# Another order for the first LayerNorms, v's products and the PSUM banks of an encoder layer on Trainium2

## The chip, the cores and the metric

The kernel runs on one core of a Trainium2 chip. The metric is the device time of one execution in microseconds (us), the median of several runs. The engines are TensorE (PE; its weight loads are listed as PEld), VectorE (DVE), ScalarE (ACT), GpSimd (POOL) and SyncE (SP), which issues nearly all of the DMAs. Each engine works through its own queue in order.

## The reference

One layer of a hybrid encoder on 1024 tokens of 1024 channels, all in fp32. What matters here is the beginning:

```python
h = layer_norm(x, emb_ln_g, emb_ln_b)
proj = h @ w_in                                 # [1024, 1024] x [1024, 5120]
q, k, v, z_a, u, z_b, g_a, g_b = split(proj)
attn = neighbourhood_attention(q, k, v, rpb)    # 8 heads x 64, window 8 x 16 on a 16 x 64 grid
u = centred_depthwise_conv(u, conv_w, conv_b)
h_lru = rg_lru(u, forward) + rg_lru(u, backward)
m = sigmoid(g_a + b0) * ((attn * silu(z_a)) @ w_ba) + sigmoid(g_b + b1) * ((h_lru * silu(z_b)) @ w_bb)
out = layer_norm(ALPHA * h + m @ w_out, ln_g, ln_b)
```

## The kernel before

Every product is done in fp32r with both operands split into a high and a low part: high x high, low x high, high x low, three matmuls for one. The order of the instructions is written out by hand for every engine: each queue gets its instructions in the order of the program text, and waits are put in where tiles are shared. So a line moved in the text moves all of its instructions in their queues.

The 1024 tokens are 8 tiles x0 to x7 of 128 tokens. A tile goes through these helpers, named as in the text:

- `load_x(i)`, `load_wv(c)`, `qk_load(m)`: DMAs, in SP's order, for x, for v's weights and for a 128-column block of the q and k weights.
- LayerNorm of tiles 0, 1 and 3: `ln_stats`, `ln_root` (a square root on ScalarE), then `ln_v(i, c)` for each half on VectorE, which reads the scale and offset straight from four PSUM banks `gps`. There they are spread over all partitions by `gb_spread`, 16 transposes of the column `gb_col`; that column comes from a transpose of the row `gb_row` (L409) and a ScalarE copy (L410). Tiles 2 and 4 to 7 take `ln_scale(i)` on ScalarE and `ln_g(i)` on GpSimd, four half-width operations, with the scale and offset copied from PSUM to SBUF by `gb_copy` on ScalarE.
- `turn(i, kk)`: four TensorE transposes (L270) of one half of tile i into a PSUM bank; `turn_hi` (L279, ScalarE) writes the high part of the turned block, `turn_lo` (L128, VectorE) the low part.
- `wv_hi(k)` (L195, ScalarE), `wv_lo(k)` (GpSimd): high and low part of chunk k of v's weights; `qk_prep(m)`: the same for q's weights (L171 on ScalarE, then GpSimd).
- `v_part(i, kind, ks)` (L328): v's products for tile i; kind "h" is high x high, "a" low x high, "w" high x low of the chunks `ks`. 24 of them make a tile's v. `v_hi` (L335) and `v_lo` read the result out, `v_store` stores it.
- `q_part(m, n)`: 24 products of a block of q; `q_hi` (L355, ScalarE) and `q_lo` (L360, VectorE) read it out. The block q(0,0) is special: its first 256 columns are computed early and its last 256 after v3, into the same bank, so the bank is held all that while.
- `t_full`, `t_last`, `t_hi`, `t_lo`: sums of turned blocks of tiles 4 to 7 for a Strassen-like scheme used later (product names a11, s2 and so on); VectorE, ScalarE and GpSimd.
- `warm_up(n)`: n idle products (L202) of a zero tile, which write into the bank `clock`; the three numbers of `WARM` say how many stand where.

The results of `turn`, `v_part` and `q_part` use four PSUM banks in this stage, and `bank(name)` hands them out in the order in which it is called:

```python
places = itertools.chain((0, 1, 2, 3, 0, 1, 2, 0, 2, 3, 1), itertools.cycle((2, 3, 0, 1)))
...
return ps0.tile([P, HALF], F32, tag=f"b{next(places)}", bufs=1, name=name)
```

A tile that gets a bank waits until the tile before it in that bank has been read for the last time. The turned blocks of tiles 2 to 7 use four other banks, which are the `gps` banks released.

The stage after it, unchanged in the text, is this (q(0,0)'s read-out and v4 are close to its end):

```python
    q_part(0, 0, slice(256, HALF))
    t_last(4)
    tile_in(5)
    q_hi(0, 0)
    ...
    tile_lo(5)
    q_lo(0, 0)
    q_store(0, 0)
    keep(7)
    q_part(1, 0)
    t_full(5)
    ...
    for kind in "hwa":
        v_part(4, kind, KS)
```

Then come v5 to v7, the rest of q, a softplus polynomial of `lru_lambda` on VectorE with one Exp on ScalarE (L629), and 16 pairs of column blocks, seven products each (up to about 424 us), with the convolution, the gates and the scans beside them; then attention, merge and output.

Of the kernel before, what the change touches and what calls it, by code (L numbers as in the profile page):

```python
# [28 lines left out]
N_PAIR = 16  # L29


WARM = 18, 4, 6
CONV_AT = (7, 24, 45, 66)
GATE_AT = (14, 24, 35, 45, 56, 66, 77, 87)
LATE_AT = (102, 102, 103, 104, 105)
# [32 lines left out]
def encoder_kernel(ctx, tc, x, gb1, gb, w_qk, w_v, w_s, w_ba, w_bb, w_gate, smalls, bias, w_out, out):  # L68
    nc = tc.nc
    V, A, G, PE, SP = nc.vector, nc.scalar, nc.gpsimd, nc.tensor, nc.sync  # L70
# [12 lines left out]
    hb12 = pool("hb12", "right")  # L83

    turns = []
    places = itertools.chain((0, 1, 2, 3, 0, 1, 2, 0, 2, 3, 1), itertools.cycle((2, 3, 0, 1)))

    def bank(name):
        if turns:
            return banks[0].tile([P, HALF], F32, tag=next(turns[0]), bufs=2, name=name)  # L90
        if banks[0] is ps0:
            return ps0.tile([P, HALF], F32, tag=f"b{next(places)}", bufs=1, name=name)
        return banks[0].tile([P, HALF], F32, tag="bank", name=name)
# [12 lines left out]
    ident = cst.tile([P, P], F32, name="ident")  # L106
# [20 lines left out]
    def lo_of(eng, lo, full, hi):  # L127
        eng.tensor_tensor(lo, full, hi.bitcast(F32), ALU.subtract)  # L128
# [28 lines left out]
    gb_row = hts[2].tile([16, P], F32, tag="ht1h", name="gb_row")  # L157
    gb_col = hts[2].tile([P, 16], F32, tag="ht1l", name="gb_col")
    zero = wsp.tile([P, P], mybir.dt.bfloat16, tag="a21", name="zero")
    V.memset(zero[:], 0.0)  # L160
    clock = bank("clock")
# [7 lines left out]
    def qk_hi(m):  # L169
        qk_w[m] = pair(wpl, [P, NK, P], f"wqk{m}", tag="w", bufs=2)  # L170
        A.copy(qk_w[m][0][:], qk_s[m][:])  # L171

    def qk_lo(m):
        hi, lo = qk_w[m]
        lo_of(G, lo[:], qk_s.pop(m)[:], hi[:])

    def qk_prep(m):
        qk_hi(m)
        qk_lo(m)
# [3 lines left out]
    def load_x(i):  # L183
        xs[i] = ln.tile([P, D], F32, tag="x", bufs=5, name=f"x{i}")
        if i == 0:
            for sl in halves:
                SP.dma_start(xs[i][:, sl], x[i][:, sl])
        else:
            SP.dma_start(xs[i][:], x[i])
# [4 lines left out]
    def wv_hi(k):  # L194
        A.copy(wv[0][k][:], wvs[k // 4][:, k % 4, :])  # L195

    def wv_lo(k):
        lo_of(G, wv[1][k][:], wvs[k // 4][:, k % 4, :], wv[0][k][:])

    def warm_up(n):  # L200
        for _ in range(n):
            PE.matmul(clock[:, :P], zero[:], zero[:], start=True, stop=True)  # L202

    gps = [[psg.tile([P, HALF], F32, name=f"gps{z}{c}") for c in range(2)] for z in range(2)]
    halves = [slice(c * HALF, (c + 1) * HALF) for c in range(2)]

    def gb_spread(z, c):

        for k in range(4):
            r = 8 * z + 4 * c + k  # L210
            PE.transpose(gps[z][c][:, k * P:(k + 1) * P], gb_col[:, r:r + 1].to_broadcast([P, P]), ident[:])

    def gb_copy(z, c):
        A.copy(gb_t[z][c][:], gps[z][c][:])

    def ln_stats(i):
        st, mv, e = (ln.tile([P, n], F32, tag=f"ln{n}{c}", bufs=2, name=f"ln{i}{c}")
                     for n, c in ((12, "t"), (2, "m"), (4, "e")))
        sts[i] = st, mv, e[:, 3:4], e[:, 0:3]
        sd, ve = sts[i][2:]  # L220
        for c in range(2):
            V.bn_stats(st[:, 6 * c:6 * c + 6], xs[i][:, halves[c]])
        V.bn_aggr(mv[:], st[:].rearrange("p (c s) -> p c s", c=2))
        V.tensor_scalar(ve[:, 0:1], mv[:, 1:2], EPS, -0.5, ALU.add, ALU.mult)

    def ln_root(i):
        st, mv, sd, ve = sts[i]
        A.activation(sd, mv[:, 1:2], AF.Sqrt, bias=eps_t[:])

    def ln_sums(i):  # L230
        ln_stats(i)
        ln_root(i)

    def ln_rstd(i):
        st, mv, sd, ve = sts[i]
        V.reciprocal(sd, sd)
        V.tensor_scalar(ve[:, 1:2], sd, sd, ve[:, 0:1], ALU.mult, ALU.mult)
        V.tensor_scalar(sd, ve[:, 1:2], 1.5, sd, ALU.add, ALU.mult)

    def ln_v(i, c):  # L240

        z, (st, mv, sd, ve), sl = xs[i], sts[i], halves[c]
        V.scalar_tensor_tensor(z[:, sl], z[:, sl], mv[:, 0:1], gps[0][c][:], ALU.subtract, ALU.mult)
        if c == 0:
            ln_rstd(i)
        V.scalar_tensor_tensor(z[:, sl], z[:, sl], sd, gps[1][c][:], ALU.mult, ALU.add)

    def ln_scale(i):

        z, (st, mv, sd, ve) = xs[i], sts[i]  # L250
        ln_rstd(i)
        V.tensor_scalar(ve[:, 2:3], mv[:, 0:1], -1.0, sd, ALU.mult, ALU.mult)
        A.activation(z[:], z[:], AF.Identity, bias=ve[:, 2:3], scale=sd)

    def ln_g(i):
        z = xs[i]
        for c in range(2):
            for w, op in enumerate((ALU.mult, ALU.add)):
                G.tensor_tensor(z[:, halves[c]], z[:, halves[c]], gb_t[w][c][:], op)

    def keep(i):
        SP.dma_start(h_d[i], xs[i][:])
# [3 lines left out]
    def turn(i, kk):  # L266
        tp = tps[i, kk] = bank(f"tp{i}_{kk}")
        for k4 in range(4):
            k = 4 * kk + k4
            PE.transpose(tp[:, k4 * P:(k4 + 1) * P], xs[i][:, k * P:(k + 1) * P], ident[:])  # L270

    def ti(i):
        return slice((i % 4) * P, (i % 4 + 1) * P)

    def tp4(i, kk):
        return tps[i, kk][:].rearrange("p (k t) -> p k t", k=4)

    def turn_hi(i, kk):
        A.copy(blocks[kk][i // 4][0][:, :, ti(i)], tp4(i, kk))  # L279

    def turn_lo(i, kk):
        hi, lo = blocks[kk][i // 4]
        lo_of(V, lo[:, :, ti(i)], tp4(i, kk), hi[:, :, ti(i)])
# [38 lines left out]
    def v_part(i, kind, ks):  # L322

        if i not in vos:
            vos[i], vn[i] = bank(f"v{i}"), 0
        for k in ks:
            a = blocks[k // 4][i // 4][kind == "a"][:, k % 4, ti(i)]
            PE.matmul(vos[i][:], a, wv[kind == "w"][k][:], start=vn[i] == 0, stop=vn[i] == 23)  # L328
            vn[i] += 1
# [3 lines left out]
    def v_hi(i):  # L333
        vs = outs["v", i] = ln.tile([P, H, 2, DH], F32R, tag="vs", bufs=2, name=f"vs{i}")
        A.copy(vs[:, :, 0, :], vos[i][:].rearrange("p (h d) -> p h d", d=DH))  # L335
# [11 lines left out]
    def q_part(m, n, cols=slice(0, HALF)):  # L347
        if (m, n) not in qos:
            qos[m, n] = bank(f"q{m}_{n}")
        run(mm3(qos[m, n][:, cols], [([t[:, 4 * kk + k, :] for t in qk_w[m]], [t[:, k, cols] for t in blocks[kk][n]])  # L350
                                     for kk in range(2) for k in range(4)]))
# [41 lines left out]
    K0, K1, KS, BOTH = range(4), range(4, 8), range(8), range(2)  # L393
# [12 lines left out]
    SP.dma_start(sm[:], smalls)  # L406

    warm_up(WARM[0])
    PE.transpose(clock[:, 256:272], gb_row[:], ident[:16, :16])  # L409
    A.copy(gb_col[:], clock[:, 256:272])  # L410
    warm_up(WARM[1])
    for z, c in ((0, 0), (1, 0), (0, 1), (1, 1)):
        gb_spread(z, c)
    warm_up(WARM[2])
    ln_sums(0)
    ln_v(0, 0)
    turn(0, 0)
    warm_up(WARM[2])
    wv_hi(0)
# [2 lines left out]
    ln_v(0, 1)  # L422
    keep(0)
    load_x(5)
    turn(0, 1)
    warm_up(WARM[2])
    wv_hi(2)
    wv_hi(3)
    turn_hi(0, 1)
    turn_lo(0, 0)  # L430
    gb_copy(0, 0)
    wv_hi(4)
    wv_hi(5)
    ln_sums(1)
    turn_lo(0, 1)
    wv_hi(6)
    wv_hi(7)
    gb_copy(1, 0)
    for k in KS:
        wv_lo(k)  # L440
    qk_prep(0)
    for k in K0:
        v_part(0, "h", (k,))
        v_part(0, "a", (k,))
    v_part(0, "w", (0, 1))
    v_part(0, "h", (4, 5))
    v_part(0, "w", (2, 3))
    v_part(0, "h", (6, 7))
    v_part(0, "a", K1)
    ln_v(1, 0)  # L450
    ln_v(1, 1)
    keep(1)
    qk_load(1)
    load_x(6)
    turn(1, 0)
    turn_hi(1, 0)
    v_part(0, "w", (4, 5))
    v_part(1, "h", K0)
    turn(1, 1)
    for z in BOTH:  # L460
        gb_copy(z, 1)
    turn_hi(1, 1)
    v_part(0, "w", (6, 7))
    ln_stats(2)
    turn_lo(1, 0)
    ln_root(2)
    v_hi(0)
    ln_scale(2)
    turn_lo(1, 1)
    ln_g(2)  # L470
    v_part(1, "w", K0)
    v_part(1, "h", K1)
    v_part(1, "a", KS)
    v_part(1, "w", K1)
    ln_sums(3)
    q_part(0, 0, slice(0, 256))
    ln_v(3, 0)
# [525 lines left out]
    for slot in range(7 * N_PAIR + 4):  # L1003
        p, k = divmod(slot, 7)
# [183 lines left out]
    for unit in range(-NT, H * NT + PV_LAG):  # L1188
        h, c = divmod(unit, NT)
# [162 lines left out]
    for i in range(NT):  # L1352
        last = i == NT - 1
        load_z(i + 3)
        z = zs.pop(i)
# [115 lines left out]
```

## Time and profile before

| | us |
|---|---|
| median of 3 runs (678.39 to 678.75) | 678.40 |
| the profiled execution | 678.46 |
| its span in the profile | 676.7 |
| TensorE busy | 665.2 (98%) |
| VectorE / ScalarE / GpSimd busy | 492.7 / 364.5 / 355.8 |
| first product of v starts | 9.99 |
| q's first half ends | 26.48 |
| first product of v4 starts | 49.19 |

All times in the rows are counted from the start of the span. A row of a timeline or of the chain gives start, duration, engine, source line, operation, tiles (out<-in, buffer numbers left out), and in brackets the idle time of that engine just before and what ended it. Matmuls are pipelined, so the durations of neighbours overlap and their pace is read from group lengths.

### The profile page before, as it was taken

How to read it: one execution, taken by the hardware profiler on the slowest of the kernel's cores; microseconds unless marked ns; L12 is line 12 of the kernel's file. 1: busy time of each engine (PE TensorE's matmuls, PEld its weight loads, DVE VectorE, ACT ScalarE, POOL GpSimd, SP SyncE). 2: the span in 40 equal slices, each digit the busy share in tenths (PEclk: the TensorE clock that was granted, in tenths of full speed). 3: DMA queues.
4: the chain of work that ended last, by engine and by line, in shares of the span. 5: the costliest groups of instructions: out<-in, count | busy, mean ns of one | idle time of the engine just before them, and what ended most of it. 6: DMA issues, size and time to landing. Idle time of an engine off the chain costs nothing.

```text
span 676.7 us, 9344 instructions
## 1 busy us (share of the span) xinstructions
PE 665.2 (98%) x3201; PEld 555.7 (82%) x3201; DVE 492.7 (73%) x821; ACT 364.5 (54%) x612; POOL 355.8 (53%) x258
## 2 busy tenths in 40 slices
PE   8999999999999999999999999999999999999995
PEld 6888888888888887888788888888888878888884
DVE  6978747886998699879967785477787787443434
ACT  6554433256786676669576634477777554210110
POOL 6798632434677576567647444116155456334442
PEclk9999999999999999999999999999999999999998
DMA  8654353233434133431553456998793467412211
GB/s 326 244 179 170 122 206 126 77 110 123 125 128 144 40 103 115 170 126 48 195 178 122 173 191 254 316 366 296 255 323 132 162 220 281 178 62 94 93 63 62
DMA packets 48702, 113.39 MB, mean 168 GB/s; under 512 B 5056, under 2 KB 9744, under 8 KB 47120
## 3 DMA queue, kind: packets, MB, share of 16 engines
q1 hardware_dynamic: 48624, 112.81, 47.2%
q8 instruction: 25, 0.41, 0.3%
q14 instruction: 21, 0.17, 0.1%
q10 hardware_dynamic: 32, 0.01, 0.0%
HBM read 77.11 MB, written 35.68 MB: 167 GB/s over the span
## 4 chain that ended last, share of the span: by engine, by line
PE 89%; DVE 6%; DMA 2%; issue 1%; SPq 1%; ACT 0%; POOL 0%; DVEq 0%; POOLq 0%
PE a L134 30%; PE o L134 13%; PE mb L134 12%; PE s L134 11%; PE q L134 6%; PE v L328 6%; PE acc L1107 3%; PE s L1061 3%; PE pt L1083 3%; PE g L759 2%; DMA wqk_s<-in_w_qk_dram 2%; DVE ws_l L128 1%; PE tp L270 1%; DMA rsb<-rs_d 1%; DVE uc L717 1%
## 5 line engine op out<-in xcount | busy, mean ns | idle before, releaser
L134 PE MATMUL o<-wo_h,ml 128*128 128x512 f32 (+1 forms) x136 | 51.2, 377 | 0.0
L134 PE MATMUL o<-wo_l,mh 128*128 128x512 f32 (+1 forms) x136 | 51.2, 376 | 0.0
L134 PE MATMUL o<-wo_h,mh 128*128 128x512 f32 (+1 forms) x136 | 51.2, 376 | 0.0
L134 PE MATMUL a<-ht_h,ws_h 128*128 128x512 f32 x128 | 50.0, 390 | 0.0
L134 PE MATMUL a<-ht_l,ws_h 128*128 128x512 f32 x128 | 49.8, 389 | 0.0
L134 PE MATMUL a<-ht_h,ws_l 128*128 128x512 f32 x128 | 49.8, 389 | 0.0
L134 PE MATMUL a<-b_h,wa_h 128*128 128x512 f32 x128 | 49.8, 389 | 0.0
L134 PE MATMUL a<-b_h,wa_l 128*128 128x512 f32 x128 | 49.8, 389 | 0.0
L134 PE MATMUL a<-b_l,wa_h 128*128 128x512 f32 x128 | 49.8, 389 | 0.0
L1071 DVE CUSTOM_DVE_ANT_0 sc<-s,bias 128x384 f32<-128x384 f32 (+1 forms) x64 | 33.4, 522 | 21.6 <-PE s L1061 14.2
L1361 DVE SCALAR_TENSOR_TENSOR z<-z,o 128x512 f32<-128x512 f32 (+1 forms) x17 | 11.2, 656 | 51.0 <-PE o L134 51.0
L1091 ACT CAST pt_h<-pt 128x384 fp32r<-128x384 f32 x64 | 29.0, 453 | 25.3 <-PE pt L1083 17.3
L1371 POOL TENSOR_TENSOR z<-z,gb 128x1024 f32<-128x1024 f32 x7 | 16.8, 2400 | 48.5 <-ACT z L1370 48.5
L1076 ACT ACTIVATE p<-sc,summ 128x384 f32<-128x384 f32 (+1 forms) x64 | 37.8, 591 | 5.5 <-DVE summ L1071 5.3
L1340 ACT ACTIVATE sd<-mv,eps_z 128x1 f32<-128x1 f32 x8 | 2.4, 294 | 67.1 <-DVE mv L1366 67.1
L128 DVE TENSOR_TENSOR pt_l<-pt,pt_h 128x384 fp32r<-128x384 f32 x64 | 33.2, 519 | 2.1 <-ACT pt_h L1091 1.6
L328 PE MATMUL v<-wv,b_h 128*128 128x512 f32 x128 | 32.9, 398 | 0.6 <-ACT b_h L279 0.5
L867 POOL CAST wb_h<-wb 128x512 fp32r<-128x512 f32 x9 | 7.0, 779 | 47.4 <-DMA wb<-in_w_bb_dram 47.4
L1061 PE MATMUL s<-ks,qs 128*128 128x384 f32 (+1 forms) x128 | 31.4, 327 | 0.0
L1083 PEld LDWEIGHTS pt<-ident,p 128*128 128x128 f32 x176 | 23.1, 140 | 8.5
L1083 PE MATMUL pt<-ident,p 128*128 128x128 f32 x176 | 29.6, 272 | 0.0
L128 POOL TENSOR_TENSOR wb_l<-wb,wb_h 128x512 fp32r<-128x512 f32 x16 | 22.0, 1375 | 14.3 <-ACT wb_h L865 13.6
(438 smaller groups left out, 2204.2 us busy)
## 6 DMA issues: line engine op xcount, KB each, us to landing
ks<-k_d SPq DMA_DIRECT2D x8, 1024.0 KB, 7.5
h_d<-x SPq DMA_DIRECT2D x8, 512.0 KB, 5.0
v_d<-vs SPq DMA_DIRECT2D x8, 512.0 KB, 3.7
q_d<-q SPq DMA_DIRECT2D x8, 512.0 KB, 3.1
ga_d<-ga SPq DMA_DIRECT2D x16, 256.0 KB, 2.2
gb_d<-gb SPq DMA_DIRECT2D x16, 256.0 KB, 2.6
k_d<-k SPq DMA_DIRECT2D x8, 512.0 KB, 3.4
qs<-q_d SPq DMA_DIRECT2D x8, 512.0 KB, 5.5
```

The source lines that it names most:

```text
L128: eng.tensor_tensor(lo, full, hi.bitcast(F32), ALU.subtract)
L134: PE.matmul(o, a, b, start=first and i == 0, stop=last and i == len(prods) - 1, skip_group_check=not (first and last))
L328: PE.matmul(vos[i][:], a, wv[kind == "w"][k][:], start=vn[i] == 0, stop=vn[i] == 23)
L759: PE.matmul(o[:, n, :], w[:, 2 * d + b, :], us[b][:, n * HALF:(n + 1) * HALF], start=z == 0, stop=z == 1)
L1061: PE.matmul(o[:, :P * len(near(t))], q[:, t * P:(t + 1) * P], k[:, z, keys], start=z == 0, stop=z == 1)
L1071: V.tensor_tensor_reduce(s[:, :w], o[:, :w], heads[h][2][:, b0:b0 + w], -1.0, 3.0e38, ALU.add, ALU.min, accum_out=sums[h][0][:, t:t + 1])
L1076: A.activation(probs[h % 2][t][:], scs.pop((h, t))[:, :w], AF.Exp, bias=sums[h][0][:, t:t + 1], scale=-1.0, accum_out=sums[h][1][:, t:t + 1])
L1083: PE.transpose(tp[:, n * P:(n + 1) * P], probs[h % 2][t][:, z * P:(z + 1) * P], ident[:])
L1091: A.copy(pt[0][:, span(b)], tps[h, b][:, :P * len(near(b))])
L1107: PE.matmul(acc[g][:, d:d + w], vvs[h // 2][:, b, h % 2, :], pt[:, a:a + w], start=b in (1, 6) and z == 0, stop=z == 1 and b == (4, 7)[g])
L1361: V.scalar_tensor_tensor(z[:, cols], z[:, cols], ALPHA * TWICE, o, ALU.mult, ALU.add)
L1371: G.tensor_tensor(z[:], z[:], gb2[:, 0, :], ALU.mult)
```

## The change

Only the head of the kernel's text is edited. The idle products become 22, 6 and 6 instead of 18, 4 and 6, one group of 6 is dropped, and the transpose of the scale's row goes to one of the `gps` banks instead of the bank of the idle products. Two of v's products for tile 0 move ahead of the second transpose of that tile; the others are put in an order that follows the arrival of the weight chunks. `ln_stats(1)` and `ln_root(1)`, `turn_lo(0, 1)`, `qk_prep(0)`, the four `gb_copy`s, `ln_stats(2)`, `ln_root(2)` and `v_hi(0)` stand elsewhere. As the calls of `bank` now come in another order, `places` is another list, and the cycle behind it is (0, 3, 2, 1) instead of (2, 3, 0, 1). Lines below the head move down by 4 (L629 becomes L633).

```diff
-WARM = 18, 4, 6
+WARM = 22, 6, 6
...
-    places = itertools.chain((0, 1, 2, 3, 0, 1, 2, 0, 2, 3, 1), itertools.cycle((2, 3, 0, 1)))
+    places = itertools.chain((0, 1, 2, 3, 0, 1, 3, 0, 3, 2, 1), itertools.cycle((0, 3, 2, 1)))
...
     warm_up(WARM[0])
-    PE.transpose(clock[:, 256:272], gb_row[:], ident[:16, :16])
-    A.copy(gb_col[:], clock[:, 256:272])
+    PE.transpose(gps[1][1][:, :16], gb_row[:], ident[:16, :16])
+    A.copy(gb_col[:], gps[1][1][:, :16])
     warm_up(WARM[1])
...
     load_x(5)
+    v_part(0, "h", (0, 1))
     turn(0, 1)
-    warm_up(WARM[2])
     wv_hi(2)
     wv_hi(3)
     turn_hi(0, 1)
     turn_lo(0, 0)
-    gb_copy(0, 0)
+    ln_stats(1)
     wv_hi(4)
+    ln_root(1)
     wv_hi(5)
-    ln_sums(1)
-    turn_lo(0, 1)
     wv_hi(6)
     wv_hi(7)
-    gb_copy(1, 0)
     for k in KS:
         wv_lo(k)
-    qk_prep(0)
-    for k in K0:
-        v_part(0, "h", (k,))
-        v_part(0, "a", (k,))
-    v_part(0, "w", (0, 1))
-    v_part(0, "h", (4, 5))
-    v_part(0, "w", (2, 3))
-    v_part(0, "h", (6, 7))
-    v_part(0, "a", K1)
+    v_part(0, "h", (2, 3))
+    v_part(0, "a", K0)
+    v_part(0, "w", (0, 1, 2))
+    v_part(0, "h", (4,))
+    v_part(0, "w", (3,))
+    v_part(0, "h", (5,))
+    v_part(0, "w", (4,))
+    v_part(0, "h", (6,))
     ln_v(1, 0)
+    turn_lo(0, 1)
     ln_v(1, 1)
     keep(1)
     qk_load(1)
     load_x(6)
     turn(1, 0)
     turn_hi(1, 0)
-    v_part(0, "w", (4, 5))
+    qk_prep(0)
+    turn_lo(1, 0)
+    v_part(0, "h", (7,))
+    v_part(0, "a", K1)
+    v_part(0, "w", (5,))
     v_part(1, "h", K0)
     turn(1, 1)
-    for z in BOTH:
-        gb_copy(z, 1)
-    turn_hi(1, 1)
-    v_part(0, "w", (6, 7))
     ln_stats(2)
-    turn_lo(1, 0)
     ln_root(2)
-    v_hi(0)
+    turn_hi(1, 1)
+    gb_copy(0, 0)
+    gb_copy(1, 0)
     ln_scale(2)
     turn_lo(1, 1)
+    gb_copy(0, 1)
+    gb_copy(1, 1)
     ln_g(2)
     v_part(1, "w", K0)
+    v_part(1, "a", K0)
+    v_part(0, "w", (6, 7))
     v_part(1, "h", K1)
-    v_part(1, "a", KS)
     v_part(1, "w", K1)
+    v_part(1, "a", K1)
+    v_hi(0)
     ln_sums(3)
```

More of the change, by code (lines that the diff above doesn't have):

```diff
@@ L456, in encoder_kernel @@
     turn_hi(1, 0)
-    v_part(0, "w", (4, 5))
+    qk_prep(0)
[3 more added lines that the diff above has]
+    v_part(0, "w", (5,))
     v_part(1, "h", K0)
     turn(1, 1)
-    for z in BOTH:
-        gb_copy(z, 1)
+    ln_stats(2)
+    ln_root(2)
     turn_hi(1, 1)
-    v_part(0, "w", (6, 7))
-    ln_stats(2)
-    turn_lo(1, 0)
-    ln_root(2)
-    v_hi(0)
+    gb_copy(0, 0)
+    gb_copy(1, 0)
     ln_scale(2)
     turn_lo(1, 1)
+    gb_copy(0, 1)
+    gb_copy(1, 1)
     ln_g(2)
     v_part(1, "w", K0)
+    v_part(1, "a", K0)
+    v_part(0, "w", (6, 7))
     v_part(1, "h", K1)
-    v_part(1, "a", KS)
     v_part(1, "w", K1)
+    v_part(1, "a", K1)
+    v_hi(0)
     ln_sums(3)
```

## The prediction

> **What bounds the kernel now.** I read the page first, then the chain that ended last in order of time, then TensorE's timeline over the first 60 us with the idle time ahead of each row, and last the other engines' timelines around the places that the change touches.
>
> ```profile
> span 676.7 us, 9344 instructions
> PE 665.2 (98%) x3201; PEld 555.7 (82%) x3201; DVE 492.7 (73%) x821; ACT 364.5 (54%) x612; POOL 355.8 (53%) x258
> ...
> PE 89%; DVE 6%; DMA 2%; issue 1%; SPq 1%; ACT 0%; POOL 0%; DVEq 0%; POOLq 0%
> ```
>
> TensorE is busy for 98% of the span and 89% of the chain. So an edit counts by what it does to TensorE's gaps: a gap closed for good shortens the run, a new one lengthens it. The profiled execution took 678.46 us, 1.76 more than its span; the median of the three runs is 678.40, so the sum below is made on 678.46 and 0.06 is taken off.
>
> The chain in order of time, cut to the stage that is edited and what follows:
>
> ```profile
> 4.68 10.67 DMA wqk_s<-in_w_qk_dram
> 15.37 1.05 ACT wqk_h L171
> 16.95 1.19 PE v L328 x4
> ...
> 23.61 2.88 PE q L134 x24
> 26.48 1.75 PE tp L270 x16
> 28.23 9.16 PE v L328 x40
> ...
> 49.35 5.44 PE v L328 x24
> ```
>
> From 16.95 on the chain is TensorE alone. The prices: a product of v 5.44/24 = 0.227 us, one of q with 256 columns 2.88/24 = 0.12, a transpose 1.75/16 = 0.11.
>
> **Part 1, the head up to 26.5 us.** WARM, the new home of the scale's transpose, the order of the LayerNorms and v's parts all lie here. TensorE's rows at the start, with the vector rows that hand it the first block:
>
> ```profile
> 1.05 2.10 PE L202 MATMUL clock<-zero 128*128 128x128 bf16 x18 [1.05 <-DVE zero L160]
> 3.40 0.25 PE L409 MATMUL clock<-ident,gb_row 16*128 16x16 f32 x1 [0.24 <-DMA gb_row<-in_gb_dram]
> 3.91 0.58 PE L202 MATMUL clock<-zero 128*128 128x128 bf16 x4 [0.26 <-ACT gb_col L410]
> 4.29 3.20 PE L211 MATMUL gps<-ident,gb_col 128*128 128x128 f32 x16
> 6.88 0.75 DVE L246 SCALAR_TENSOR_TENSOR x<-x,ln0e,gps 128x512 f32<-128x512 f32 x1
> 7.68 0.66 PE L270 MATMUL tp<-ident,x 128*128 128x128 f32 x4
> 8.17 0.50 PE L202 MATMUL clock<-zero 128*128 128x128 bf16 x6
> ...
> 9.99 0.48 PE L328 MATMUL v<-wv,b_h 128*128 128x512 f32 x1
> ...
> L202 PE MATMUL clock<-zero x40: 219/300/314, 1.0 to 10.0; 128*128 128x128 bf16 x40
> ```
>
> A slow idle product comes every (2.10 - 0.31)/17 = 0.105 us, with the 0.31 of one such matmul (the last row's longest) taken off. 22 of them are issued by 1.05 + 22 x 0.105 = 3.36, just ahead of the scale's row at 3.40; the next six no longer wait for the scalar copy, because the transpose has left their bank, so the 16 spreads start near 4.1 instead of 4.29. The two gaps of 0.24 and 0.26 go. Nothing comes of it: x's first half is finished by the vector engine at 6.88 + 0.75 = 7.63, and the first transposes start at 7.68 either way. A rule of the Trainium skill speaks for this edit: "TensorE: Matmul & The Clock Gate", Part 1, says that about 3.4 us of sustained activity open the clock, so that closing the gaps could open it one window earlier; the spreads would then run at double speed, but by the row at 7.68 that too is waiting time.
>
> From the first product of v at 9.99 to the end of q's first half TensorE issues 48 products of v, 8 transposes and 24 products of q: 48 x 0.227 + 8 x 0.11 + 2.88 = 14.7 us. The stretch to 26.48 is 16.5 long, so 1.8 us of it is waiting. The new order can close a part of that: two products of v stand where six idle ones stood, and `turn_hi(1,0)` now stands ahead of `qk_prep(0)`, so TensorE no longer waits for the cast at 15.37, which itself waited for a DMA. How much it closes I need not know, because what follows is held by another transfer:
>
> ```profile
> 26.21 1.06 ACT L171 CAST wqk_h<-wqk_s 128x1024 fp32r<-128x1024 f32 x1 [1.98 <-DMA wqk_s<-in_w_qk_dram]
> 27.17 1.06 ACT L279 CAST b_h<-tp 128x512 fp32r<-128x512 f32 x2
> 28.12 0.30 ACT L228 ACTIVATE ln4e<-ln4m,eps_t 128x1 f32<-128x1 f32 x1
> 28.32 1.07 ACT L279 CAST b_h<-tp 128x512 fp32r<-128x512 f32 x2
> ...
> 28.46 0.16 DVE L236 RECIPROCAL ln4e<-ln4e 128x1 f32<-128x1 f32 x1
> ```
>
> ScalarE's `qk_prep(1)` waits 1.98 us for w_qk's second tile and its queue is in order: behind it stand the casts of tiles 2 and 3. The fifth product of `v_part(2)`, at about 28.23 + 4 x 0.227 = 29.1, needs the cast that runs from 28.32 to about 28.9: at most 0.2 us is free. The DMA is queued behind x5 and the store of x1, which no edit moves. So whatever the head saves is gone by 29.1, and I cost the head at 0 (bounds: 0.2 faster; and not slower, as long as it slips by less than the wait of part 2, which would swallow it). That covers the `gb_copy`s too: they now stand right ahead of `ln_g(2)`, and should GpSimd, and with it `turned_in(2, 1)`, come some tenths late for them, those tenths end in the same wait.
>
> **Part 2, `places`.** This edit outlives the head. Counting the calls of `bank`, before: clock 0, tp0 1 and 2, v0 3, tp1,0 0, v1 1, tp1,1 2, q(0,0) 0, v2 2, v3 3, q(1,0) 1, and from the cycle v4 2, v5 3, v6 0, v7 1. After: clock 0, tp0,0 1, v0 2, tp0,1 3, tp1,0 0, v1 1, tp1,1 3, q(0,0) 0, v2 3, v3 2, q(1,0) 1, then v4 **0**, v5 3, v6 2, v7 1. So v4 goes into the bank of q(0,0) instead of v2's. The built instruction stream says the same: v4's first product waits for `q_lo(0,0)` (L360), not for `v_lo(2)`. When is that?
>
> ```profile
> 39.80 0.69 DVE L128 TENSOR_TENSOR vs<-v,vs 128x512 fp32r<-128x512 f32 x1 [1.78 <-ACT vs L335]
> ...
> 46.35 0.69 DVE L302 TENSOR_TENSOR t<-tp,b_h 128x512 f32<-128x512 f32 x1 [1.83 <-ACT t L301]
> ...
> 51.86 1.66 DVE L310 TENSOR_TENSOR t<-t,b_l 128x512 f32<-128x512 f32 x1
> ...
> 54.64 0.67 DVE L360 SCALAR_TENSOR_TENSOR q<-q,q 128x512 fp32r<-128x512 f32 x1
> ...
> 49.19 0.62 PE L328 MATMUL v<-wv,b_h 128*128 128x512 f32 x2
> ```
>
> v2's bank was free at 39.80 + 0.69 = 40.49, 8.7 us before TensorE asked for a bank at 49.19. q(0,0)'s is read until 54.64 + 0.67 = 55.31. A semaphore costs 0.05 (7.63 to 7.68 above), so v4 starts at 55.36: **6.17 us** of standing still, in TensorE's in-order queue, with all later products behind it. VectorE cannot be earlier: from 46.35 it works without a pause up to L360, and its work from 28.46 on follows the ScalarE queue pinned in part 1. Nothing lends the time back, since TensorE has no other gap of that size later in which to catch up.
>
> **Part 3, a moved wait at the softplus.** The built stream of the changed kernel differs once more outside the head: the wait of ScalarE's Exp (L629) for VectorE's L628 now stands ahead of its table load instead of behind it, since the other banks and buffers give Exp a second wait.
>
> ```profile
> 1.19 1.28 ACT L114 ACT_TABLE_LOAD   x1 [1.19 <-PEq L1455]
> 2.48 0.20 ACT L114 ACTIVATE warm<-eps_t 128x1 f32<-128x1 f32 x1
> ...
> 106.73 1.28 ACT L629 ACT_TABLE_LOAD   x1
> 108.44 0.21 ACT L629 ACTIVATE sp<-sp 128x8 f32<-128x8 f32 x1 [0.42 <-DVE sp L628]
> ...
> 108.23 0.17 DVE L628 TENSOR_TENSOR sp<-sm,sp 128x8 f32<-128x8 f32 x1
> 108.68 0.17 DVE L630 TENSOR_SCALAR sp<-sp 128x8 f32<-128x8 f32 x1 [0.27 <-ACT sp L629]
> ...
> 120.79 0.68 DVE L658 TENSOR_TENSOR up<-u,a 128x512 f32<-128x512 f32 x1
> ...
> 121.72 0.39 PE L134 MATMUL a<-ht_h,wa_h 128*128 128x512 f32 x1
> ```
>
> Before, the load was done at 108.01, while VectorE still worked. Now it starts at 108.44 and Exp at 109.72, 1.28 later; VectorE has no further pause up to L658, so that ends at 121.47 + 1.28. The product at 121.72 needs it (0.05 behind its end, 0.20 to spare): **1.08 us** more, relative to a TensorE that is late already (bounds 0, if a pause hides it, and 1.28). "ScalarE: Activation LUTs", *What ACT_TABLE_LOAD costs*, in the Trainium skill adds a drain of 1.38 us to every load; by it this term would be 2.5. The trace disagrees: the first load of all ends at 2.47 and its ACTIVATE starts at 2.48, so the row stands.
>
> **Part 4, the clock after the wait.** Standing still for 6 us may cost the full clock. The trace shows both directions:
>
> ```profile
> 668.44 0.28 PE L134 MATMUL o<-wo_l,mh 128*128 128x256 f32 x1
> ...
> 672.00:673.00 1.00, 0.00 (x0) 0.00 (x0) 1.00 (x4) 0.00 (x0) 0.00 (x0) 0.76 0.00 0
> 673.00:676.00 3.00, 0.00 (x0) 0.00 (x0) 0.65 (x2) 0.00 (x0) 0.00 (x0) 0.50 0.53 175
> ```
>
> Idle products come every 0.105 us at the start and every (0.50 - 0.22)/5 = 0.056 at 8.17: half clock, then full, a factor of 1.9. At the end the last matmul is over at 668.72, and the granted clock (the third figure from the right) falls to half at about 672.5: 0.76 over that us, 0.50 after it; 3.8 us without work sufficed, and this wait is 6.1. Half clock loses 0.47 us per us until it rises. Before the rise near 6.9 lay 5.85 us of work with two gaps, or 3.0 us without one: 2.75 or 1.4 us lost; if the clock holds, 0. I take **2.1**, the middle of the two that the rows give. By the same Part 1 of the Trainium skill the clock is gated by free-running windows of 3.4 us; a wait of 6.1 then holds a whole idle window in (6.1 - 3.4)/3.4, some 8 of 10, starts. The row at 672 agrees that one such window is enough.
>
> **The sum.** 678.46 + 0 + 6.17 + 1.08 + 2.1 = 687.8; less 0.06 and rounded, **687.8 us**.
>
> **Rivals.**
> *The clock holds.* Parts 2 and 3 alone: 678.40 + 7.25 = 685.7. For it: only one such fall is in the trace. Against: 6.1 is well over 3.8. 0.15.
> *The bank is not waited for* (q(0,0) is read out in time, or the change doesn't do to the banks what the count says) and the table load is hidden: the pinned cast leaves 678.3, no change. For it: v4's bank was free 8.7 us early before, so there is a margin that some other order could keep. Against: the count and the built stream agree, and VectorE would have to be 6 us earlier. 0.05.
> *Faster: the head's gain goes through.* If w_qk's second tile came sooner, so that the casts at 27.17 and 28.32 moved forward with the transposes, and VectorE with them past L360, up to the 1.8 us of waiting before 26.48 could be kept: 676.6. It decides only if that DMA lands over 1 us before 26.2 and v4 finds its bank free, so it needs two things that the rows deny. 0.03.
> The forecast itself: 0.72. The last 0.05: other prices in the same direction (684 or 691).
>
> **How the numbers follow.** Low end: part 2 alone, 684.6, so 684.5. High end: 6.17 + 1.28 + 2.75 = 10.2, 688.6, with nearly 1 us for a slower re-start: 689.5. The forecast and the first rival lie inside, 0.87 together, less what their own bounds miss. A measurement of this kernel tells about 0.2% (1.4 us) from no change; faster by more 0.03, within 0.05, slower 0.92.
>
> **What the profile after would show.** Right: one row of L328 near 55 us with an idle of 5 to 6.5 us before it, released by DVE q L360; matmuls of 512 columns coming every 0.43 us instead of 0.227 for some us after it and a granted clock under 1 there; a table load of L633 near 117 that starts behind VectorE, and some 1 us of idle on TensorE a dozen us on, released by DVE up; the head's waits at 16.95 gone; all later stages shifted by a constant. Wrong: no wait ahead of v4, or a bank wait that ends well before 55, or TensorE's L328 rows of v2 starting over 0.5 us before 28.

## The result, and the profile after

The changed kernel takes **688.09 us** (median of 4 runs, 686.65 to 689.40) against 678.42 for the kernel before in the same comparison: ratio 1.0141, 95% interval [1.0124, 1.0158]. In a later comparison four runs gave 687.64 (687.34 to 687.97) against 678.74, ratio 1.0128 [1.0114, 1.0141]. It is slower by 8.9 to 9.7 us.

The first lines of the page, and the share of the chain by engine:

```profile
span 687.6 us, 9345 instructions
PE 667.8 (97%) x3201; PEld 557.8 (81%) x3201; DVE 489.2 (71%) x821; ACT 364.1 (53%) x612; POOL 354.5 (52%) x258
...
PE 82%; DVE 12%; DMA 2%; issue 2%; ACT 1%; SPq 0%; POOL 0%; DVEq 0%; ACTq 0%; POOLq 0%
```

TensorE issues the same 3201 products, but VectorE's share of the chain has doubled: somewhere TensorE now follows VectorE. The table of TensorE's waits says where (us in total, times, longest):

```profile
PE v L328 <- DVE q L360: 5.9, 1, 5.9
PE v L328 <- ACT b_h L279: 1.9, 1, 1.9
PE clock L202 <- DVE zero L160: 1.0, 1, 1.0
PE a L134 <- DVE up L662: 1.0, 1, 1.0
PE v L328 <- POOL wv L128: 0.5, 1, 0.5
PE v L328 <- DVE b_l L128: 0.5, 1, 0.5
```

The first row is v4's wait for q(0,0)'s bank. The fourth is the softplus that came late. The others lie in the head. The chain in order of time shows what the waits do to the stages behind them:

```profile
56.58 8.08 PE v L328 x24
65.53 5.49 PE v L328 x24
...
82.79 32.66 PE q L134 x144
...
552.80 39.50 PE mb L134 x172
592.31 87.36 PE o L134 x408
```

The 24 products of v4 take 8.08 instead of 5.44 us, those of v5 again 5.49. The 144 products of q start 9.86 later than before (72.93), the merge 10.92 later (541.88), the output 10.94 later (581.37). Nearly all is lost ahead of 82.79, and a smaller part, 1.06, behind it. Of the 9.86, 1.32 is there before the wait begins: the products ahead of v4 end at 50.67 (56.58 - 5.91) instead of 49.35, because the head of this execution came late (see *The head at 0* below).

VectorE and ScalarE around the two waits (start, duration, engine, line, operation, tiles, idle before and its releaser):

```profile
47.52 0.69 DVE L302 TENSOR_TENSOR t<-tp,b_h 128x512 f32<-128x512 f32 x1 [1.83 <-ACT t L301]
...
55.76 0.67 DVE L360 SCALAR_TENSOR_TENSOR q<-q,q 128x512 fp32r<-128x512 f32 x1
...
118.11 0.17 DVE L632 TENSOR_TENSOR sp<-sm,sp 128x8 f32<-128x8 f32 x1
119.89 0.17 DVE L634 TENSOR_SCALAR sp<-sp 128x8 f32<-128x8 f32 x1 [1.61 <-ACT sp L633]
```
```profile
118.35 1.28 ACT L633 ACT_TABLE_LOAD   x1 [1.77 <-DVE sp L632]
119.64 0.21 ACT L633 ACTIVATE sp<-sp 128x8 f32<-128x8 f32 x1
```

L360 ends at 56.43, and v4 starts 0.15 later. The table load stands behind VectorE's L632 instead of beside it, and VectorE loses 1.61 us to it where it lost 0.27.

The windows around the first wait; the figure behind POOL's is the granted clock:

```profile
50.00:54.00 4.00, 0.67 (x3) 0.21 (x2) 3.93 (x6) 1.66 (x3) 3.92 (x3) 1.00 0.28 94
54.00:57.00 3.00, 0.42 (x1) 0.45 (x2) 2.43 (x4) 0.62 (x1) 3.00 (x4) 0.63 0.59 225
57.00:60.00 3.00, 3.00 (x8) 2.32 (x8) 1.08 (x2) 1.09 (x2) 2.47 (x2) 0.50 0.78 300
60.00:61.00 1.00, 1.00 (x4) 0.71 (x4) 0.97 (x3) 0.00 (x0) 0.00 (x0) 0.50 0.39 148
61.00:62.00 1.00, 1.00 (x5) 0.82 (x4) 1.00 (x3) 0.00 (x0) 0.00 (x0) 0.69 0.00 0
62.00:63.00 1.00, 1.00 (x6) 0.82 (x5) 0.96 (x3) 0.00 (x0) 0.00 (x0) 1.00 0.00 0
```

A mean of 0.63 over 3 us is 2.22 us at half clock, so it fell at 54.78; 0.69 in the us from 61 puts the rise at 61.62. In between, v's products start 0.43 us apart instead of 0.227 (of the 8 that touch the 3 us from 57, one had started before them).

### The profile page after: what moved, and what is told of

It reads as the page before. It is cut to its first block, busy times and chain, and to the rows that moved or that the text cites. A ratio compares the mean times of both kernels' runs of the same rounds, so it can differ in the third digit from the quotient of the medians.

```text
span 687.6 us, 9345 instructions
## 1 busy us (share of the span) xinstructions
PE 667.8 (97%) x3201; PEld 557.8 (81%) x3201; DVE 489.2 (71%) x821; ACT 364.1 (53%) x612; POOL 354.5 (52%) x258
## 4 chain that ended last, share of the span: by engine, by line
PE 82%; DVE 12%; DMA 2%; issue 2%; ACT 1%; SPq 0%; POOL 0%; DVEq 0%; ACTq 0%; POOLq 0%
PE a L134 27%; PE o L134 13%; PE mb L134 12%; PE s L134 10%; PE q L134 5%; PE v L328 4%; PE acc L1111 3%; PE s L1065 3%; PE pt L1087 3%; PE g L763 2%; DMA x<-in_x_dram 1%; DVE ws_l L128 1%; DVE b_l L128 1%; DVE wa_l L128 1%; DMA rsb<-rs_d 1%
## 5 line engine op out<-in xcount | busy, mean ns | idle before, releaser
L328 PE MATMUL v<-wv,b_h 128*128 128x512 f32 x128 | 35.1, 421 | 8.9 <-DVE q L360 5.9
L328 PEld LDWEIGHTS v<-wv,b_h 128*128 128x128 f32 x128 | 25.0, 202 | 15.6 <-issue 6.3
```

## The experiments

The theory: the bank that `places` gives to v4 is the whole loss, through three terms (the wait, the half clock that it causes, the Exp), and the new head is worth nothing, because w_qk's second tile holds ScalarE. Rivals: the head itself is a gain or a loss, the terms are not separate, or the DMA is not what holds the head.

**The bank alone, put into the kernel before.**

```diff
-    places = itertools.chain((0, 1, 2, 3, 0, 1, 2, 0, 2, 3, 1), itertools.cycle((2, 3, 0, 1)))
+    places = itertools.chain((0, 1, 2, 3, 0, 1, 2, 0, 2, 3, 1), itertools.cycle((0, 3, 2, 1)))
```

> The kernel before with one edit: the cycle of places is (0, 3, 2, 1), so that v4 takes the bank of q(0,0). Everything else is the kernel before. Theory: the whole loss of the change is here, with all three terms: about 6.2 us of wait ahead of v4, 1.1 us behind the table load, 0 to 3 us of half clock: 687.8 us, 685.7 to 688.6. Rival (half of the loss is the head's): 682 to 684.

Measured: 688.89 us (688.54 to 689.07), ratio 1.0152 [1.0139, 1.0166] to the kernel before, 678.55. Its waits, of TensorE:

```profile
PE v L328 <- DVE q L360: 6.0, 1, 6.0
...
PE a L134 <- DVE up L658: 1.0, 1, 1.0
```

Two numbers swapped in a tuple of banks make the whole loss, the Exp's wait included, with the old head; a loss of which half is the head's is refuted. The median lies 0.3 above the expected range (688.6) and 0.8 to 1.25 above the changed kernel's two. Against the second profile of the changed kernel (55.51 and 7.58, see *The clock* below) this run's profile has v4 0.35 later and the 24 products of v4 0.50 slower, and both differ from one execution to the next.

**The bank alone, taken out of the changed kernel; first try.**

```diff
-    places = itertools.chain((0, 1, 2, 3, 0, 1, 3, 0, 3, 2, 1), itertools.cycle((0, 3, 2, 1)))
+    places = itertools.chain((0, 1, 2, 3, 0, 1, 3, 0, 3, 2, 1), itertools.cycle((3, 2, 0, 1)))
```

> The changed kernel with one edit: the cycle of places is (3, 2, 0, 1), so that v4 takes the bank of v2, as before the change, and not that of q(0,0). The head is the changed one. Theory (the bank decides, the head is held by the DMA of w_qk's second tile): no wait ahead of v4, no fall of the clock; in the built stream the wait of the softplus Exp is back behind its table load, so that term goes too: 678.4 us, within 0.5. Rival A (the head itself costs, since its DMAs landed 1.1 to 1.3 us later in the changed kernel's profile): about 679.5. Rival B (the head gains and the bank only hid it): 676.6 to 677.6.

Measured: 680.10 us (678.98 to 681.01) against 678.55, ratio 1.0022 [1.0013, 1.0031]: 1.2 above the upper end of what the theory expected. v4's wait is gone, but the run doesn't settle what the head is worth, since the cycle set up a new wait at its far end, where the first product of the pairs gets a bank after q(3,1):

```profile
PE a L134 <- DVE q L360: 1.4, 1, 1.4
```

**The same, with that end kept too.** v4 goes into v2's bank and q(3,1) into bank 3, as in the kernel before; the rest of the change stays.

```diff
-    places = itertools.chain((0, 1, 2, 3, 0, 1, 3, 0, 3, 2, 1), itertools.cycle((0, 3, 2, 1)))
+    places = itertools.chain((0, 1, 2, 3, 0, 1, 3, 0, 3, 2, 1, 3, 2, 0, 1), itertools.cycle((2, 3, 0, 1)))
```

> The changed kernel with four more places written out and the old cycle behind them, so that v4 goes into v2's bank, as in the kernel before, and q(3,1) into bank 3, not into bank 2. Everything else of the change (WARM, the LayerNorms' order, v's parts) stays. In the built stream v4 waits for the last read of v2, and the softplus's Exp waits behind its table load. My theory (the bank of v4 is the whole loss, the head is worth nothing because w_qk's second tile holds ScalarE): 678.4, between 677.9 and 678.9, no wait of TensorE for L360 and none for the vector product at the a banks. Rival, the head is a gain that the bank hid: 676.6 to 677.6. Rival, the head is itself a loss: 679.3 or more.

Measured: 678.33 us (677.75 to 679.04, 11 runs) against 678.74, ratio 0.9992 [0.9984, 1.0001]. All that TensorE waits for at 0.3 us or more is in the head, but for one wait that the kernel before has too (w L792):

```profile
PE clock L202 <- DVE zero L160: 1.0, 1, 1.0
PE v L328 <- POOL wv L128: 1.0, 2, 0.5
PE a L134 <- DVE w L796: 0.4, 1, 0.4
PE v L328 <- ACT b_h L279: 0.3, 1, 0.3
PE tp L270 <- DVE x L246: 0.3, 1, 0.3
```

The loss is gone, and without it the rest of the change is worth between 1.1 us less and 0.1 more. Of the rival by which it was a gain of 1 us or more hardly anything is left, of the one by which it was a loss nothing. Beside the changed kernel once more on the same chip:

> The changed kernel once more beside the three others on one chip, so that their differences to it are paired: 688.1, between 686.6 and 689.4. The gap to the kernel with v4 in v2's bank is what the bank costs; my theory says all of it, 9.4 to 10.

Measured: 687.64 us (687.34 to 687.97). The bank costs 687.64 - 678.33 = 9.3 us, just under the 9.4 to 10 expected.

**The clock alone.** Idle products fill the wait ahead of v4; they write to a bank that is free.

```diff
+    clock2 = ps0.tile([P, HALF], F32, tag="b3", bufs=1, name="clock2")
+    for _ in range(96):
+        PE.matmul(clock2[:, :P], zero[:], zero[:], start=True, stop=True)
```

> The changed kernel with 96 more idle products of the zero tile ahead of v4's first product, in the bank that v2 has left, so that TensorE works through most of the wait. At 0.056 us each they fill 5.4 of about 6 us and add nothing behind it. Theory: v4 starts as late as in the changed kernel, but the granted clock stays full: the half clock's 1.4 to 2.75 us go, 685.7 us, and the spread between executions shrinks. Rival (the half clock costs nothing, the wait alone makes the time): 688, as the changed kernel.

Measured: 685.53 us (684.56 to 686.33), ratio 1.0101 [1.0086, 1.0116]. TensorE's timeline with the filling, in which v4 still can't start before L360 has ended:

```profile
49.96 5.53 PE L565 MATMUL clock<-zero 128*128 128x128 bf16 x96
56.16 3.89 PE L328 MATMUL v<-wv,b_h 128*128 128x512 f32 x16 [0.67 <-DVE q L360]
```

Busy without use, but at full clock afterwards: 16 products in 3.89. That is worth 688.09 - 685.53 = 2.6 against the first runs of the changed kernel, 687.64 - 685.53 = 2.1 against the second. That the spread would shrink is not shown: it is 1.8 us here, and was 2.75 and 0.6 in the changed kernel's two sets of four runs.

**The Exp alone.** An Exp of a constant ahead of the softplus loads the table early.

```diff
+    A.activation(warm[:], eps_t[:], AF.Exp)
     V.tensor_scalar(smh[:], sm[:], 0.5, None, ALU.mult)
```

> The changed kernel with one more Exp of a 128x1 constant ahead of the softplus stage on ScalarE, which brings the table load forward, out from behind the wait for VectorE. Theory: the load runs beside VectorE's work again, the 1.0 us that TensorE waits for up (L658 of the kernel before) goes: 687.1 us by the median, 1.0 under the changed kernel. Rival (that wait would be replaced by another at the same place): 688, as the changed kernel.

Measured: 686.34 us (685.08 to 686.70), ratio 1.0112 [1.0098, 1.0126]: 1.3 to 1.75 below the two medians of the changed kernel. The wait for `up` is gone from the table. The gain is above the 1.0 expected, and this run doesn't isolate it: its profile, of the fastest of the four runs, also has v4 start 0.6 us earlier than the changed kernel's second profile (54.90 against 55.51) and a smaller cost of the clock (next section).

**Both together.**

> The changed kernel with both additions at once: the idle products ahead of v4 keep the clock full, and the early Exp of a constant takes the table load off the softplus's wait. What is left of the loss is the wait for q(0,0)'s bank alone. If the terms of the sum are what they were taken for and add up: 678.6 + 5.5 to 6.2 = 684.1 to 684.8, about 1.1 below the run with the idle products alone (685.5), with a full clock from 7 us to the last stage and no wait for the vector product at the a banks. Rival, the two terms are one (a late VectorE seen twice) or the early load costs elsewhere: 685.3 or more.

Measured: 684.63 us (683.97 to 685.04) against 678.77, ratio 1.0088 [1.0074, 1.0102]. TensorE waits 0.6 for L360 behind the 96 idle products, and for `up` no more. What is left is 5.9 us, about the wait of 5.9 to 6.0 for the bank. The two terms are two, and they add up: from the run with the idle products alone the early Exp takes 0.90 by the medians, or 1.1 if each is set against the kernel before that ran beside it (678.55 and 678.77).

**What holds the head.** The kernel with v4 in v2's bank, and w_qk's second tile ahead of x5 and of the store of x1 on SP's queue:

```diff
     keep(0)
-    load_x(5)
...
-    keep(1)
     qk_load(1)
+    load_x(5)
+    keep(1)
     load_x(6)
```

> The same kernel with w_qk's second tile fetched ahead of x's sixth block and the store of x1 on SyncE's queue, which takes away the DMA that holds ScalarE's cast. If that DMA is what keeps the head's gain from going through: 677.8, between 677.3 and 678.1, 0.5 to 0.6 below the run without this edit, with ScalarE's pause ahead of L171 gone (the rest of the gain is then held by GpSimd's work on the LayerNorms). If something else holds it: the same time as without the edit, within 0.2.

Measured: 678.34 us (677.40 to 678.75), ratio 0.9989 [0.9981, 0.9998], the same as without the edit (678.33). ScalarE without it, then with it:

```profile
26.21 1.05 ACT L171 CAST wqk_h<-wqk_s 128x1024 fp32r<-128x1024 f32 x1 [2.17 <-DMA wqk_s<-in_w_qk_dram]
27.17 1.07 ACT L279 CAST b_h<-tp 128x512 fp32r<-128x512 f32 x2
```
```profile
24.61 1.05 ACT L171 CAST wqk_h<-wqk_s 128x1024 fp32r<-128x1024 f32 x1 [0.33 <-DMA wqk_s<-in_w_qk_dram]
27.00 1.08 ACT L279 CAST b_h<-tp 128x512 fp32r<-128x512 f32 x2 [1.34 <-PE tp L270]
```

The DMA did hold the cast: it now starts 1.6 us earlier. But the cast behind it comes only 0.17 earlier, and waits for the transposes instead. They run from 26.37 without a pause, straight behind q's first half. GpSimd's `ln_g(2)` (21.65 + 5.29 = 26.94) doesn't hold them, though the expectation had it so: the four transposes that need its last half are the ninth to twelfth of the 16, and with 0.11 for one they start at 27.24. What TensorE follows up to there is the start of the head, as the chain of this run shows:

```profile
1.65 6.00 DMA wvsh<-in_w_v_dram
...
18.62 5.03 PE v L328 x22
23.66 2.88 PE q L134 x24
...
28.28 9.13 PE v L328 x40
```

The DMA brings v's first weights; behind it stand ScalarE's cast and GpSimd's low parts of them. The head was held at two places at nearly the same time, this one and w_qk's second tile, so lifting one shows nothing. The expectation of 0.5 to 0.6 was wrong: the limit behind the DMA was nearer than that. The control, with the same move in the kernel before:

> The control: the kernel before with the same move on SyncE's queue and nothing else. If the earlier DMA helps only together with the new order of the head: 678.4, within 0.2 of the kernel before. If the DMA alone held the kernel before: 677.9 or less.

Measured: 678.56 us (678.18 to 678.86), ratio 0.9996 [0.9987, 1.0005]: no difference, as expected. No version is faster than the kernel before by the 0.2% that the prediction set as the bound: the two best are at 0.9989, its interval just below 1, and 0.9992, which is 0.5 to 0.8 us. That w_qk's second tile sets how much of a gain gets through is seen in the run with the early Exp, though not by an edit: there the cast behind it starts at 25.71, 0.50 earlier than in the kernel before, and the products ahead of v4 end at 48.88, 0.47 earlier (49.35).

## Why the prediction was right, step by step

The forecast was 687.8, and the medians are 688.09 and 687.64. The changed kernel's profiles show v4's wait, the half clock and the wait for `up`; the steps don't all carry equally well, and that the sum comes within 0.3 us is partly luck (see *The sum*).

*The head at 0.* Right up to the end of this stage. The chain of the kernel with the bank put right shows how the saving dies:

```profile
23.42 2.88 PE q L134 x24
28.04 9.36 PE v L328 x40
40.13 2.86 PE q L134 x24
```

It reaches q's first half 0.19 earlier than the kernel before (23.61), starts v2 0.19 earlier (28.23), needs 9.36 for the 40 products instead of 9.16, and is level at 40.13 (40.12) and still at the 144 products of q (72.94 against 72.93). That is the pinned cast at work, as predicted. The 0.5 us (-0.1 to 1.1) that the ratio gives, above the bound of 0.2, is not the head's in these profiles, which differ by 0.7: 0.2 of it falls near 263 us, where a group of 24 products takes 5.44 instead of 5.74 in every profile with the new head (why stays open), and 0.5 ahead of the merge, at two DMAs that follow each other (1.80 and 3.49 us instead of 1.58 and 4.22; 1.75 and 3.54 in the last experiment's control, which has the old head).

The reason was incomplete: the prediction names one DMA alone. The head hangs on an earlier one too, and its saving depends on it. The table shows when ScalarE's first cast of v's weights starts (L195, it waits for a DMA), and when the transposes of tiles 2 and 3 start (L270 x16):

| profile | first cast, us | transposes, us | between, us |
|---|---|---|---|
| kernel before | 6.22 | 26.32 | 20.10 |
| kernel before, other bank cycle | 8.09 | 26.86 | 18.77 |
| kernel before, w_qk's tile earlier | 8.48 | 27.17 | 18.69 |
| changed, early Exp | 6.55 | 25.24 | 18.69 |
| changed, again | 7.44 | 26.12 | 18.68 |
| changed, both additions | 8.51 | 27.17 | 18.66 |
| changed, first profile | 8.99 | 27.67 | 18.68 |

The other four profiles with the new head lie at 18.66 to 18.69 as well. So up to here the new head follows the landing of v's first weights, as far as eight profiles show it; no run here moves that DMA. Where they land early it is over 1 us faster than the old head, where they land at 8 us or later the two agree within 0.1. The landing differs by over 2 us between executions, with either head, so this is a spread that a bound on one execution has to hold.

The other half of the bound, "not slower", failed in the first profile for that reason. The argument for it, that the wait of part 2 would swallow a slip, doesn't hold: VectorE slips with the head, L360 ends at 56.43 instead of 55.31, and the wait stays as long. The prediction's side sum for the spreads was off as well (they start at 4.34, not near 4.1, behind six idle products), but the first transposes start at 7.73, close to the 7.68 that it counted on.

*The bank, 6.17.* Right. The wait was 5.91 and 6.03 us in the two profiles, 6.02 with only the cycle changed, and 5.9 us are left in the median when the other two terms are taken away. The trace counts it from the end of the last product (49.35 in the kernel before), the prediction from the start of the next, which overlaps that end (49.19); this makes 0.16 of the difference. The start at 55.36 was 55.51 in the second profile.

*The Exp, 1.08.* Right. The waits are 1.0 and 1.1, the merge and the output slip by 1.06 more, and the pair of runs that differ in this alone gives 0.9 to 1.1. The load ends at 118.35 + 1.28 = 119.63 and its ACTIVATE starts at 119.64, with no gap between them. "ScalarE: Activation LUTs", *What ACT_TABLE_LOAD costs*, in the Trainium skill adds a drain of 1.38 us to the load; these rows don't show one. The 2.5 that it would have made is refuted.

*The clock, 2.1.* The size was right, but as a middle of what varies. Four executions with the wait, each with the 24 products of v4 from its chain (the changed kernel, again, with the early Exp, the kernel before with the cycle alone):

```profile
56.58 8.08 PE v L328 x24
```
```profile
55.51 7.58 PE v L328 x24
```
```profile
54.90 7.22 PE v L328 x24
```
```profile
55.86 8.08 PE v L328 x24
```

They can't be set against the 5.44 of the kernel before, where the first product overlaps the one ahead of it. The run with the idle products has a wait of 0.67 ahead of v4 too, but at full clock:

```profile
56.16 5.71 PE v L328 x24
```

So 0.27 us is a re-start, which the prediction had only in its high end (at nearly 1 us), and the clock cost 2.37, 1.87, 1.51 and 2.37: all within the 1.4 to 2.75 that two rows of the profile before had given. The clock fell in every one; the rival in which it holds is refuted.

*The sum.* Partly luck. The first profile, 689.40 us, has 1.32 of late head, 5.91 of wait and 2.64 of re-start and half clock, 9.87 by v5; its output starts 10.94 later than before, and 678.46 + 10.94 = 689.40. The second, 687.34 us, has 0.13, 6.03 and 2.14, 8.30 by v5, and 8.89 by the output (590.26). The forecast had 9.35 in all, without the late head and the re-start, and without what later stages give back, such as the 0.2 near 263. The later stages shift as a whole, and the wait at 16.95 is gone, as foretold; in the head's new order other waits stand there (0.5 for GpSimd, 0.5 for VectorE).

## What to carry to other kernels

Where tiles rotate through a few banks by a list, any edit that adds, drops or reorders a call shifts all later places: count the calls, and look for the holder that lives longest (here a block computed in two halves), because the next tile behind it stands still until its last read. Count to the very end of the rotation as well: the first repair here moved the collision to the last block of q. And before a head is tuned, look for all the places at which it is held, since lifting one of two nearly equal limits shows nothing.

## What the runs showed of the hardware

A wait of 6 us cost more than its length, by an amount that depends on where it falls against the windows of the clock. The granted clock around v4 in the second profile, then with the early Exp, then with the cycle alone in the kernel before; the rows in which it falls and rises:

```profile
52.00:53.00 1.00, 0.00 (x0) 0.00 (x0) 1.00 (x1) 0.00 (x0) 1.00 (x2) 0.83 1.03 349
...
59.00:60.00 1.00, 1.00 (x5) 0.75 (x4) 0.97 (x3) 0.00 (x0) 0.00 (x0) 0.75 0.32 123
```
```profile
50.00:52.00 2.00, 0.00 (x0) 0.00 (x0) 1.97 (x3) 0.79 (x2) 1.92 (x2) 0.83 0.38 130
...
58.00:59.00 1.00, 1.00 (x5) 0.81 (x4) 0.97 (x2) 0.00 (x0) 0.00 (x0) 0.93 0.71 274
```
```profile
54.00:55.00 1.00, 0.00 (x0) 0.00 (x0) 1.00 (x2) 0.57 (x1) 1.00 (x1) 0.55 1.01 397
...
60.00:61.00 1.00, 1.00 (x4) 0.80 (x3) 1.00 (x3) 0.00 (x0) 0.00 (x0) 0.53 0.00 0
```

Worked out as above, the clock was at half from 52.66 to 59.50, from 51.32 to 58.14 and from 54.10 to 60.94, and in the first profile from 54.78 to 61.62: 6.82 to 6.84 us in all four, twice 3.42. Its place against the wait is what differs. v4 ran 3.99, 3.24, 5.08 and 5.04 us of it, and the clock cost it 1.87, 1.51, 2.37 and 2.37: 0.47 for each us at half clock, the loss that the prediction took from the pace of the idle products. "TensorE: Matmul & The Clock Gate", Part 1, in the Trainium skill has the clock judged in free-running windows of about 3.4 us, and these lengths agree. It also says that the clock closes after an idle window; here it fell 2.4 us after TensorE had stopped (54.90 - 6.02 = 48.88 to 51.32) in the run with the early Exp, and 4.1 in the first profile (50.67 to 54.78). If the fall marks the end of such a window, the one that ended at 51.32 began at 47.90, 1 us before the stop: a window that was not idle for its whole length was enough there.
